# Four slots in place of two for the gated recurrence's results, and the attention's first loads and constants queued four units later

## The chip, the cores and the metric

The kernel runs on one core of a Trainium2 chip. The metric is the device time of one execution in microseconds (us), as the median of several runs. The core has five engines with a queue each: TensorE (PE, with its weight loads shown as PEld), VectorE (DVE), ScalarE (ACT), GpSimd (POOL) and SyncE (SP). SP issues nearly all DMA transfers here. Each engine works through its queue in order.

## The reference

One layer of a streaming encoder on 2048 tokens with 16 meta tokens ahead of them, all in float32, width 1024. Cut to what matters here:

```
p  = rms_norm(h) @ w_in                    # columns: a (gated recurrence), b (attention), c (RWKV-7)
oa = rg_lru_group(xa, ya, ...)             # u = conv4(xa); r, i = sigmoid(u @ ga), sigmoid(u @ gx)
                                           # h_t = a_t h_{t-1} + sqrt(1 - a_t^2) (i u)_t;  h * gelu(ya)
ob = forgetting_attention_group(q, k, v, f_logit, ...)   # softmax(q k / 8 + c_q - c_k), causal, 8 heads
oc = rwkv7_group(pc, ...)                  # matrix-state recurrence, 4 heads of 64
h += rms_norm([oa | ob | oc] @ w_out)
h += rms_norm((gelu(g) * v) @ w_down),  [g | v] = causal_dwconv3(rms_norm(h) @ w_up)
return h without the meta tokens
```

## The kernel before

The program is written as stages, and a list scheduler orders each engine's queue from a simulated timeline, so that small edits move many instructions by a few places. `issue_after(ins)` adds one more rule to that: what is issued inside it stands behind the instruction `ins` in its engine's queue. It is no semaphore.

*Projections.* The input projection runs in three parts ("thirds") of tokens, `w_in_part`. A part has 24 units of 128 output columns, in the order c (8), a (4), k (4), v (4), q (4); each unit loads its weights (`wh`, `wl`, L260) and multiplies them in three products (L193, L194, L195) into a bank `psp`. The bank goes to `stp` (L58, L60) or, for k and q, is split into `sth` (L278) and `stl` (L279), and is stored to DRAM: `scr_p`, `scr_kh`, `scr_kl`, `scr_qh`, `scr_ql`. `core.loaded` is the weight load of the newest unit, `core.split` the newest split L279 on DVE.

*Beside them* the two recurrences run as generators, a step after each unit: the RWKV group (L1106 to L1480; its inverse of small blocks has L1288 on DVE with L1287 on POOL, and the products L1317 with the copies L1333, L1340, L1347 on DVE between) and the gated recurrence, `lru_block`. For each block of 256 tokens and each of two halves of the width `lru_block` loads `lraw` (L1550), writes `u` (tag `lu`, in the profile `rwlu`) on ACT (L1557) and three times on DVE (L1559), multiplies it with the gates, reuses it for the scan, and stores it to `scr_mix` (L1592). The tag has two slots, so a `u` may be written when the store of the `u` two before it has landed. Also beside them, `up_sums` (L1805 loads, sums on POOL, L1811 stores `us`) and, in the middle third, W_out's split.

*The attention* starts when the last third is projected. Its maxima (L645 into `mx`, L650 on DVE into `mc`, L657 `sh`, L660) come first, then the scores (L774, L775). Some of its setup is queued early, in the last third, after a mark set by `SETTLED`: in the loop over units `i` is 1 + the number of units done, one more after the gate's unit,

```
if part == 2 and i == SETTLED:
    core.settled, core.parted = core.loaded.ins, core.split.ins
```

`core.settled` stands on SP's queue: behind it come the loads of the first two heads' keys (`keys`, L605 to L610; only L605 of each can go at once, since the others wait for other tiles or data) and the first three loads of queries (L632). `core.parted` stands on DVE's queue: behind it come the fills of constant rows in these tiles (`fixed`: L567 four times, L559, L560 and L561 three times each). After the attention come W_out and the feed-forward, up and down.

Of the kernel before, what the change touches and what calls it, by code (L numbers as in the profile page):

```python
# [18 lines left out]
P = 128  # L19
# [1516 lines left out]
def lru_block(core, R, scr, k, b):  # L1536

    nc = core.nc
    t0 = max(0, Rwkv.start(b))
    n = min(T, Rwkv.start(b + 1)) - t0  # L1540
    c0 = PAD + t0
    tt = nc.vector.tensor_tensor
    stt = nc.vector.scalar_tensor_tensor

    def tl(s):
        return R.t([P, 256], s, bufs=2 if s == "lu" else 1)[:, :n]

    def raw(row, a):
        t = R.t([P, 260], "lraw", bufs=2)[:, : c0 + n - a]
        nc.sync.dma_start(t, scr["p"][row : row + P, a : c0 + n])  # L1550
        return t

    for p in range(2):
        pc = slice(p, p + 1)
        x = raw(P * p, c0 - 3)
        u, r, g, al = (tl("l" + s) for s in ("u", "r", "g", "a"))
        nc.scalar.activation(u, x[:, 3:], AF.Identity, scale=k["conv_w"][:, 6 + p : 7 + p], bias=k["conv_b"][:, pc])  # L1557
        for i in range(3):
            stt(u, x[:, i : n + i], k["conv_w"][:, 2 * i + p : 2 * i + p + 1], u, op0=ALU.mult, op1=ALU.add)  # L1559


        ps = R.pe()
        pa, px = ps[:, :n], ps[:, 256 : 256 + n]
        nc.tensor.matmul(pa, k["ga_w"][:, p], u, start=True, stop=True)
        nc.tensor.matmul(px, k["gx_w"][:, p], u, start=True, stop=True)
        nc.scalar.activation(r, pa, AF.Abs, bias=k["ga_b"][:, pc])
        nc.vector.tensor_scalar(al, pa, k["ga_b"][:, pc], 0.0, op0=ALU.add, op1=ALU.min)
        nc.scalar.activation(g, px, AF.Tanh, scale=0.5, bias=k["rate"][:, 2, pc])
        nc.scalar.activation(r, r, AF.Tanh, scale=0.5)
        nc.scalar.activation(al, al, AF.Exp)  # L1570
        stt(r, r, 1.0, al, op0=ALU.add, op1=ALU.mult)
        stt(g, g, 1.0, u, op0=ALU.add, op1=ALU.mult)
        yield
        nc.scalar.activation(al, r, AF.Exp, scale=k["rate"][:, 0, pc])
        nc.scalar.activation(r, r, AF.Tanh, scale=k["rate"][:, 1, pc])

        tt(u, al, al, op=ALU.mult)
        stt(r, u, 1.0, r, op0=ALU.add, op1=ALU.mult)
        nc.vector.tensor_scalar(r, r, 1e-34, None, op0=ALU.max)
        nc.scalar.activation(r, r, AF.Sqrt)  # L1580
        stt(g, g, 0.5, r, op0=ALU.mult, op1=ALU.mult)
        nc.vector.tensor_tensor_scan(u, al, g, k["h"][:, pc], op0=ALU.mult, op1=ALU.add)
        nc.vector.tensor_copy(k["h"][:, pc], u[:, n - 1 : n])

        ya, y = raw(2 * P + P * p, c0), r
        nc.scalar.activation(y, ya, AF.Square)
        nc.vector.tensor_scalar(y, y, 0.044715, 1.0, op0=ALU.mult, op1=ALU.add)
        tt(y, y, ya, op=ALU.mult)
        nc.scalar.activation(y, y, AF.Tanh, scale=0.7978845608028654)
        stt(y, y, 1.0, ya, op0=ALU.add, op1=ALU.mult)  # L1590
        stt(u, u, 0.5, y, op0=ALU.mult, op1=ALU.mult)
        nc.sync.dma_start(scr["mix"][P * p : P * p + P, t0 : t0 + n], u)  # L1592
        yield
# [558 lines left out]


READY = 13
SETTLED = 17
PACE = 1.25

WIDE = (0, 5)
# [63 lines left out]
def hybrid_block_kernel(ctx: ExitStack, tc: tile.TileContext, args, out):  # L2222
# [25 lines left out]
    with ExitStack() as p1:  # L2248
# [8 lines left out]
        with ExitStack() as p1a:  # L2257
# [14 lines left out]
            for part in range(3):  # L2272
# [40 lines left out]
                for whole in units:  # L2313
# [10 lines left out]
                    i += 1  # L2324
                    if part == 2 and i == SETTLED:
                        core.settled, core.parted = core.loaded.ins, core.split.ins
# [211 lines left out]
```

## Time and profile before

| | |
|---|---|
| median of 3 runs | 2940.53 us (2938.65 to 2941.93) |
| profiled execution | 2949.89 us, its span 2948.2 us |
| mean granted TensorE clock | 0.979 |
| busy in the span | PE 2844.4, DVE 2006.8, ACT 1502.3, POOL 1297.5 us |
| projections with recurrences | to about 846 us |
| attention, W_out, feed-forward | from 846 us to the end |

Times within the profile are from the start of the span. A row of the timeline has start, duration, engine, line, operation, output<-input, and in brackets how long the engine stood idle before it and what released it. A row of the waits has engine, tile and line, what it waited for, us in total, times, and the longest.

### The profile page before, as it was taken

What the parts mean: (1) busy time and instruction counts of PE and PEld (TensorE: products, weight loads), DVE (VectorE), ACT (ScalarE), POOL (GpSimd) and SP (SyncE); (2) the same over time, 40 slices, a digit from 0 to 9 for tenths busy, and PEclk for the clock granted to TensorE, in tenths of its full rate; (3) what the DMA queues carried; (4) which work ended last, traced back from release to release, by engine and by line L of the source; (5) the groups of instructions that cost most, each with busy time, mean ns of one, the idle gap of its engine ahead of it and who ended that gap; (6) DMA issues with size and microseconds to landing.
All of it is one profiled execution on the core that took longest, in us unless ns stands there. A gap on an engine that the chain in (4) does not pass through costs nothing.

```text
span 2948.2 us, 53211 instructions
## 1 busy us (share of the span) xinstructions
PE 2844.4 (96%) x18854; PEld 2446.0 (83%) x18854; DVE 2006.8 (68%) x3839; ACT 1502.3 (51%) x2937; POOL 1297.5 (44%) x1572
## 2 busy tenths in 40 slices
PE   8999999999988889999999999999999999999998
PEld 8998989888965555666578999999999999787887
DVE  4357655665678875556656988887777787556766
ACT  3246452454436654545645656666666665324333
POOL 1001222222114667677624676456655444656443
PEclk9998999999978999999999999999999999999999
DMA  7775678577643348444264665577777765436453
GB/s 241 250 245 185 215 240 291 174 241 246 204 120 77 90 115 227 97 122 129 48 192 148 212 194 179 160 233 209 219 199 222 215 198 149 141 111 218 151 170 122
DMA packets 470343, 530.51 MB, mean 180 GB/s; under 512 B 86862, under 2 KB 356888, under 8 KB 468524
## 3 DMA queue, kind: packets, MB, share of 16 engines
q1 hardware_dynamic: 469308, 526.18, 59.1%
q8 instruction: 148, 2.42, 0.4%
q0 software_dynamic: 768, 0.93, 0.1%
q14 instruction: 119, 0.97, 0.1%
HBM read 368.07 MB, written 158.90 MB: 179 GB/s over the span
## 4 chain that ended last, share of the span: by engine, by line
PE 75%; DVE 8%; DMA 6%; ACT 5%; issue 3%; POOL 2%; SPq 1%; DVEq 0%; POOLq 0%; ACTq 0%
PE psu L193 9%; PE psu L194 9%; PE psu L195 9%; PE psp L194 4%; PE psp L195 4%; PE psp L193 4%; PE psd L193 4%; PE psd L194 4%; PE psd L195 4%; PE po L797 4%; PE sc L774 2%; PE mx L645 2%; PE pswo L193 2%; PE pswo L194 2%; PE pswo L195 2%
## 5 line engine op out<-in xcount | busy, mean ns | idle before, releaser
L194 PE MATMUL psu<-xo,uw 128*128 128x344 f32 x1848 | 591.5, 320 | 0.0
L193 PE MATMUL psu<-xo,uw 128*128 128x344 f32 x1848 | 586.4, 322 | 3.0 <-DVE vb L1972 2.1
L195 PE MATMUL psu<-xo,uw 128*128 128x344 f32 x1848 | 581.9, 320 | 0.4 <-DVE uw L1781 0.3
L193 PE MATMUL psp<-xh,wh 128*128 128x384 f32 (+2 forms) x1152 | 380.4, 330 | 0.5 <-DMA wh<-scr_wk 0.5
L194 PE MATMUL psp<-xl,wh 128*128 128x384 f32 (+2 forms) x1152 | 375.3, 326 | 0.0
L195 PE MATMUL psp<-xh,wl 128*128 128x384 f32 (+2 forms) x1152 | 373.9, 325 | 0.4 <-DMA wl<-scr_wk 0.4
L1781 DVE TENSOR_TENSOR uw<-uq,uw 128x512 fp32r<-128x512 f32 x341 | 318.2, 938 | 62.5 <-ACT uw L1780 56.5
L193 PEld LDWEIGHTS psu<-xo,uw 128*128 128x128 f32 x1848 | 345.9, 188 | 5.2 <-DVE vb L1972 3.7
L194 PEld LDWEIGHTS psu<-xo,uw 128*128 128x128 f32 x1848 | 347.2, 188 | 0.0
L195 PEld LDWEIGHTS psu<-xo,uw 128*128 128x128 f32 x1848 | 345.7, 188 | 1.1 <-DVE uw L1781 1.1
L1780 ACT ACTIVATE uw<-uq 128x512 fp32r<-128x512 f32 x462 | 287.9, 627 | 95.2 <-PE psu L195 42.0
L779 ACT ACTIVATE p<-sc,bias 128x512 f32<-128x512 f32 (+4 forms) x352 | 197.6, 590 | 168.5 <-PE sc L775 147.5
L650 DVE TENSOR_REDUCE mc<-mx 128x1 f32<-128x512 f32 (+5 forms) x352 | 190.8, 566 | 110.4 <-PE mx L645 78.1
L1920 DVE SCALAR_TENSOR_TENSOR uy<-psu,ffn_cols,uy 128x342 f32<-128x342 f32 (+1 forms) x390 | 220.5, 567 | 61.9 <-ACT uy L1918 60.4
L1928 POOL TENSOR_TENSOR uy<-uy,uy 128x342 f32<-128x342 f32 (+1 forms) x132 | 145.4, 1102 | 231.5 <-ACT uw L1780 56.6
L1781 POOL TENSOR_TENSOR uw<-uq,uw 128x512 fp32r<-128x512 f32 x121 | 183.6, 1518 | 131.9 <-ACT uw L1780 108.8
L193 PEld LDWEIGHTS psp<-xh,wh 128*128 128x128 f32 x1152 | 218.9, 190 | 6.4 <-issue 3.7
L194 PEld LDWEIGHTS psp<-xl,wh 128*128 128x128 f32 x1152 | 219.0, 190 | 5.6 <-issue 4.0
L195 PEld LDWEIGHTS psp<-xh,wl 128*128 128x128 f32 x1152 | 218.9, 190 | 4.9 <-issue 2.9
L818 POOL TENSOR_TENSOR acc<-acc,p 128x512 f32<-128x512 f32 (+3 forms) x186 | 196.1, 1057 | 56.3 <-DVE acc L818 26.8
L1781 DVE TENSOR_TENSOR fo<-u,fo 128x896 fp32r<-128x896 f32 x88 | 100.6, 1143 | 131.0 <-ACT fo L1780 130.5
L1780 ACT ACTIVATE fo<-u 128x896 fp32r<-128x896 f32 x88 | 81.2, 923 | 206.7 <-PE psd L195 118.8
(492 smaller groups left out, 6309.8 us busy)
## 6 DMA issues: line engine op xcount, KB each, us to landing
uq<-scr_us SPq DMA_DIRECT2D x220, 256.0 KB
uq<-in_ffn_up_dram SPq DMA_DIRECT2D x209, 256.0 KB
wh<-scr_wk SPq DMA_DIRECT2D x48, 512.0 KB
wl<-scr_wk SPq DMA_DIRECT2D x48, 512.0 KB
u<-scr_ff SPq DMA_DIRECT2D x88, 256.0 KB
scr_ff<-uy SPq DMA_DIRECT2D x110, 171.0 KB
raw<-in_w_in_dram SPq DMA_DIRECT2D x24, 512.0 KB
scr_wk<-wh SPq DMA_DIRECT2D x24, 512.0 KB
```

The source lines that it names most:

```text
L193: nc.tensor.matmul(out, ah, bh, start=first, stop=False, skip_group_check=more)
L194: nc.tensor.matmul(out, ah, bl, start=False, stop=False, skip_group_check=more)
L195: nc.tensor.matmul(out, al, bh, start=False, stop=last, skip_group_check=more)
L645: nc.tensor.matmul(ps[:rows, : e - a], q3[:, qo : qo + rows], k2[:, a:e], start=True, stop=not last)
L650: self.reduced = nc.vector.tensor_reduce(mc[:rows, i, ci : ci + 1], ps[:rows, : e - a], axis=AX.X, op=ALU.max)
L779: last = nc.scalar.activation(p[:rows, :w], ps[:rows, :w], AF.Exp, bias=bias[:rows, j : j + 1])
L797: mm = nc.tensor.matmul(po[at : at + 64, c0:n], v1[:rows, j], p[:rows, : n - c0], start=start and i < 2, stop=end and i + 2 >= len(group), ...
L818: eng.tensor_tensor(a, ps_[0][0][:rows, c0:n] if start and i == 1 else a, p[:rows, : n - c0], op=ALU.add)
L1780: core.nc.scalar.activation(hi, src, AF.Copy)
L1781: (eng or core.nc.vector).tensor_tensor(lo, src, hi, op=ALU.subtract)
L1920: core.conved = stt(y[:, :n], src[:, i : n + i], cw[:, 44 * i + cc : 44 * i + cc + 1], y[:, :n], op0=ALU.mult, op1=ALU.add)
L1928: core.pooled = nc.gpsimd.tensor_tensor(v[:, :n], g[:, :n], v[:, :n], op=ALU.mult)
```

## The change

It has two edits: four slots for `lu` in place of two (two more tiles of 1 KB per partition), and the mark four units later, after the third v unit in place of the third k unit.

```diff
 def tl(s):
-    return R.t([P, 256], s, bufs=2 if s == "lu" else 1)[:, :n]
+    return R.t([P, 256], s, bufs=4 if s == "lu" else 1)[:, :n]
...
-SETTLED = 17
+SETTLED = 21
```

For DVE the mark moves by one unit alone, to the split of the last k unit, since v units have no split. The scheduler's order changes with it. Numbers behind names are the program's tile numbers; `k_1402` and `q_1403` to `q_1405` are the attention's tiles.

SP's queue in the middle of the last third, before:

```order
L605 DMA k_1402_11222<-scr_kh 64x1040
L632 DMA q_1404_11231<-scr_qh 64x512
L1550 DMA rwlraw_9576<-scr_p 128x256
L289 DMA scr_p<-stp_8355 128x256
L632 DMA q_1405_11235<-scr_qh 64x512
L605 DMA k_1402_11222<-scr_kh 64x1040
L632 DMA q_1403_11227<-scr_qh 64x512
L1550 DMA rwlraw_9626<-scr_p 128x259
L1592 DMA scr_mix<-rwlu_8192 128x256
```

and the same place after:

```order
L1805 DMA us_8822<-in_ffn_up_dram 128x2x128 x3
L1550 DMA rwlraw_9576<-scr_p 128x256
L289 DMA scr_p<-stp_8355 128x256
L1550 DMA rwlraw_9626<-scr_p 128x259
L1592 DMA scr_mix<-rwlu_8192 128x256
```

The two key loads and three query loads are gone from between. They stand some 35 rows further down now:

```order
L1805 DMA us_9467<-in_ffn_up_dram 128x2x128 x4
L605 DMA k_1402_11222<-scr_kh 64x1040
L632 DMA q_1404_11231<-scr_qh 64x512
L632 DMA q_1405_11235<-scr_qh 64x512
L605 DMA k_1402_11222<-scr_kh 64x1040
L632 DMA q_1403_11227<-scr_qh 64x512
L1106 DMA rwraw_9697<-scr_p 128x2x257
L282 DMA scr_kh<-sth_8861 128x256
L283 DMA scr_kl<-stl_8862 128x256
L1811 DMA scr_us<-us_9467 512x1x256
L260 DMA wh_9477<-scr_wk 128x1024
```

Behind them stand a load of the RWKV group, stores of the third k unit, a store of `us` and the weights of unit 20.

DVE's queue at the first of these places, where it takes the `rwlu` of that raw load, before:

```order
L1340 TENSOR_TENSOR rwxf_7542<-rps_7639,rwxu_7503 32x8x32 x4
L60 COPY stp_8383<-psp_8358 128x256
L1288 TENSOR_REDUCE rwix_7467<-rwitmp_7470 128x8
L1559 SCALAR_TENSOR_TENSOR rwlu_9628<-rwlraw_9626,lru_cols,rwlu_9628 128x256
L1288 TENSOR_REDUCE rwix_7467<-rwitmp_7470 128x8
L1347 COPY rwxu_7503<-rps_7704 32x256 x2
```

and after:

```order
L1340 TENSOR_TENSOR rwxf_7542<-rps_7639,rwxu_7503 32x8x32 x4
L60 COPY stp_8383<-psp_8358 128x256
L1559 SCALAR_TENSOR_TENSOR rwlu_9628<-rwlraw_9626,lru_cols,rwlu_9628 128x256
L1288 TENSOR_REDUCE rwix_7467<-rwitmp_7470 128x8
L1559 SCALAR_TENSOR_TENSOR rwlu_9628<-rwlraw_9626,lru_cols,rwlu_9628 128x256
L1347 COPY rwxu_7503<-rps_7704 32x256 x2
```

A second L1559 has come ahead of the copy L1347.

PE's queue from the last product of the projections, before:

```order
L195 MATMUL psp_10174<-xh_6612,wl_9893 128x256
L1413 MATMUL rps_9325<-rstate,rwgt_9300 64x64 x4
L1444 MATMUL rps_9363<-rstate,rwrav_7307 64x64
L1413 MATMUL rps_9325<-rstate,rwgt_9300 64x64 x4
L1444 MATMUL rps_9363<-rstate,rwrav_7307 64x64
L645 MATMUL mx_11279<-k_1402_11222,q_1404_11231 128x144
```

and after:

```order
L195 MATMUL psp_10174<-xh_6612,wl_9893 128x256
L1393 MATMUL rps_9302<-rwsc_7355,rwxu_9238 64x128 x8
L1393 MATMUL rps_9313<-rwsc_7355,rwxu_9238 64x128 x8
L1405 MATMUL rps_9325<-rww_947_7356,rwsc_7355 64x64 x16
L1413 MATMUL rps_9325<-rstate,rwgt_9300 64x64
L645 MATMUL mx_11279<-k_1402_11222,q_1404_11231 128x144
```

L1393 and L1405, which stood among the projections' products before, have come behind the last of them.

DVE's queue at the same place, up to the first L657, before:

```order
L567 CAST k_1411_11247<-ident 64x520 x4
L1454 TENSOR_REDUCE rwgsm_9362<-rps_9363 128x4
L650 TENSOR_REDUCE mc_11277<-mx_11287 128x1
L650 TENSOR_REDUCE mc_11277<-mx_11291 128x1
L1399 COPY rstate<-rstate 128x128
L1198 TENSOR_TENSOR rwrav_9803<-rwr_9796,rwe_9713 128x8x64
L1199 TENSOR_TENSOR rwrav_9803<-rwk_9706,rwe_9713 128x8x64
L1117 SCALAR_TENSOR_TENSOR rwrav_9803<-rwraw_9804,rwkv_cols,rwrav_9803 128x4x64
L1454 TENSOR_REDUCE rwgsm_9362<-rps_9383 128x4
L1117 SCALAR_TENSOR_TENSOR rwrav_9803<-rwraw_9804,rwkv_cols,rwrav_9803 128x4x64
```

and after:

```order
L1417 COPY rstate<-rps_9325 128x128
L567 CAST k_1411_11247<-ident 64x520
L650 TENSOR_REDUCE mc_11277<-mx_11283 128x1
L650 TENSOR_REDUCE mc_11277<-mx_11287 128x1
L1305 STREAM_TRANSPOSE rwxu_10009<-rwxu_10009 128x256
L1417 COPY rstate<-rps_9325 128x128
L650 TENSOR_REDUCE mc_11277<-mx_11291 128x1
L650 TENSOR_REDUCE mc_11277<-mx_11294 128x1
L657 TENSOR_REDUCE sh_11299<-mc_11277 128x4
```

Most of the recurrence's instructions there (L1198, L1199, L1117, L1454) have moved behind L657.

## The prediction

> **What bounds the kernel now.** I read the page first, for the busy times.
>
> ```profile
> PE 2844.4 (96%) x18854; PEld 2446.0 (83%) x18854; DVE 2006.8 (68%) x3839; ACT 1502.3 (51%) x2937; POOL 1297.5 (44%) x1572
> ```
>
> PE is the bound nearly everywhere: only 104 us of the 2948.2 us span (2948.2 - 2844.4) are idle on it, so an edit that touches neither a PE product nor one of those gaps is worth nothing. The windows say where PE stands still or runs at a lower granted clock. The columns are busy us with counts for PE, PEld, DVE, ACT, POOL, then PEclk, the DMA share and GB/s.
>
> ```profile
> 260.00:300.00 40.00, 34.20 (x185) 27.94 (x184) 30.03 (x62) 22.91 (x47) 7.47 (x11) 0.79 0.51 166
> 300.00:400.00 100.00, 99.58 (x944) 91.43 (x943) 62.87 (x154) 48.89 (x92) 23.51 (x37) 1.00 0.70 229
> 720.00:740.00 20.00, 15.60 (x174) 14.05 (x174) 8.27 (x25) 3.77 (x9) 4.76 (x8) 0.74 0.84 253
> 850.00:900.00 50.00, 41.30 (x269) 28.45 (x268) 34.16 (x89) 23.78 (x55) 13.34 (x23) 0.66 0.60 140
> 900.00:1050.00 150.00, 134.32 (x1407) 87.81 (x1407) 123.35 (x341) 94.91 (x208) 88.89 (x145) 0.91 0.34 85
> ```
>
> Three places lose PE time: 260 to 300, 720 to 740, and the attention's start after 850. Each also loses clock. The waits of ACT tie the first two to the slots of `lu`:
>
> ```profile
> ACT rwlu L1557 <- DMA scr_mix<-rwlu: 16.2, 6, 8.2
> ```
>
> ACT's first write of a `u` waited 16.2 us in 6 places for the store of the `u` two before it, at most 8.2 us. The timeline around that longest one, queue by queue:
>
> ```profile
> 721.67 0.53 SPq L1550 DMA_DIRECT2D rwlraw<-scr_p  x1
> 722.51 0.33 SPq L1592 DMA_DIRECT2D scr_mix<-rwlu  x1
> 722.66 0.26 DVE L1288 TENSOR_REDUCE rwix<-rwitmp 128x8 f32<-128x104 f32 x1 [2.19 <-POOL rwitmp L1287]
> 724.42 0.28 PE L194 MATMUL psp<-xl,wh 128*128 128x256 f32 x1
> 725.16 0.27 DVE L1288 TENSOR_REDUCE rwix<-rwitmp 128x8 f32<-128x112 f32 x1
> 726.96 0.60 ACT L1557 ACTIVATE rwlu<-rwlraw,lru_cols 128x256 f32<-128x256 f32 x1 [8.18 <-DMA scr_mix<-rwlu]
> 727.60 0.48 DVE L1559 SCALAR_TENSOR_TENSOR rwlu<-rwlraw,lru_cols,rwlu 128x256 f32<-128x256 f32 x1 [2.17 <-ACT rwlu L1557]
> 728.30 0.88 DVE L1347 COPY rwxu<-rps 32x256 f32<-32x256 f32 x2
> 728.77 0.31 PE L1317 MATMUL rps<-rwxf,rwxu 32*32 32x32 f32 x2 [4.08 <-DVE rwxu L1347]
> ```
>
> It reads as one chain. The store L1592 is issued at 722.51; ACT's L1557 starts at 726.96; DVE, in order, stands at L1559 until 727.60 although the copy L1347 behind it is ready; PE stands 4.08 us for that copy. The windows around it show what follows:
>
> ```profile
> 724.00:728.00 4.00, 0.69 (x7) 0.49 (x5) 1.76 (x6) 0.87 (x2) 1.77 (x4) 1.00 1.03 320
> 728.00:732.00 4.00, 3.23 (x61) 2.88 (x63) 2.62 (x8) 0.75 (x2) 0.52 (x1) 0.52 0.60 205
> 732.00:736.00 4.00, 4.00 (x26) 3.63 (x23) 1.98 (x7) 1.98 (x4) 0.00 (x0) 0.50 0.64 221
> 736.00:740.00 4.00, 4.00 (x32) 3.58 (x33) 0.17 (x1) 0.17 (x1) 0.00 (x0) 0.70 0.99 297
> 740.00:744.00 4.00, 4.00 (x42) 3.54 (x40) 2.67 (x6) 2.69 (x7) 2.65 (x4) 1.00 0.14 42
> ```
>
> After the gap PE is busy at about half clock for some 11 us.
>
> **The change, part by part.** *A, the gap at 724.* Both edits work on it. With four slots L1557 no longer needs the store of `rwlu_8192` but one two `u` older; and the two key loads and three query loads leave SP's queue ahead of the raw load `rwlraw_9626`. What is late next: the raw load itself, issued at 721.67 behind two key loads of 64 x 1040 and three query loads of 64 x 512 numbers, 904 KB, that are gone, so about 3 us sooner (904 KB at the 320 GB/s of the row above). Then L1557 (0.60) is done before 725. On DVE L1288 ends at 725.43; the new order has two L1559 (0.48 each) around it, ahead of L1347, so the copy's first half (0.44) ends at 725.43 + 0.96 + 0.44 = 726.8, and PE, which has stood since 724.69, idles 2.1 us in place of 4.08. DVE's own stand of 2.19 us at 722.66, behind POOL and a load of `us` that shared the transfers with the keys, shrinks too, by 1 us or so as I judge. So 1 us is left and 3.1 us are won. The clock: 0.48 x 3.23 + 0.50 x 4 + 0.30 x 4 = 4.75 us of PE time went at the lower clock in the three windows; with a gap of 1 us I take all of it as won, since no gap of that size is followed by a dip here (300 to 400 has 0.42 us of idle and 1.00, and PE's 0.99 us gap at 716.42 leaves 1.00):
>
> ```profile
> 716.42 1.49 PE L1317 MATMUL rps<-rwxu 32*32 32x32 f32 x96 [0.99 <-ACT stp L58]
> 716.00:720.00 4.00, 3.53 (x114) 3.41 (x115) 3.63 (x12) 2.41 (x5) 1.53 (x3) 1.00 1.12 257
> ```
>
> A = -3.1 - 4.75 = -7.8. Ends: 0 (something else is as late as the store) and -8.8 (4.08 + 4.75).
>
> [...]
>
> *B, the gap at 264 (part 0 to part 1).*
>
> ```profile
> 255.20 0.60 ACT L1557 ACTIVATE rwlu<-rwlraw,lru_cols 128x256 f32<-128x256 f32 x1 [2.21 <-DMA scr_mix<-rwlu]
> 255.83 0.48 DVE L1559 SCALAR_TENSOR_TENSOR rwlu<-rwlraw,lru_cols,rwlu 128x256 f32<-128x256 f32 x1 [1.54 <-ACT rwlu L1557]
> 269.90 0.79 PE L1232 MATMUL rps<-rwrav,rwbk 64*128 64x128 f32 x2 [5.66 <-DVE rwbk L1200]
> 270.00:275.00 5.00, 5.00 (x24) 3.04 (x24) 4.73 (x9) 0.00 (x0) 2.41 (x3) 0.50 0.91 272
> ```
>
> DVE stood 1.54 us at L1559 for the same kind of store and then works almost without a break until the L1200 that PE waits for. Without the stand the whole row moves up 1.5 us, and the PE gap becomes 4.1. That is as long as the gap of A, so I leave the dip behind it as it is: B = -1.5, with ends 0 and -8.7 (if the clock's 0.21 x 34.2 = 7.2 us in 260 to 300 were won too). The remaining 4 of the 6 waits stand in front of no PE gap: 0.
>
> *C, the keys' new place* (SP, about 762). They need about 3 us of transfer, and stand ahead of `rwraw_9697`, an `us` store, and the weights of unit 20:
>
> ```profile
> 768.93 0.38 SPq L260 DMA_DIRECT2D wh<-scr_wk  x1
> 847.97 0.34 PE L645 MATMUL mx<-k,q 128*128 128x144 f32 x1
> 772.00:776.00 4.00, 4.00 (x37) 4.00 (x37) 3.87 (x19) 0.90 (x2) 0.00 (x0) 1.00 1.02 329
> ```
>
> The first product that reads the keys stands at 847.97. The attention follows the last projection there at once, and a unit is some 11 us (part 2's last four cannot start before 802 or so if they end at 846), so unit 20 reads its weights about 30 us after their load. Both have time to spare: 0. Without that cover a late weight load would cost PE its 3 us.
>
> *D, the constants' new place.* DVE's ten fills go behind the `stl` of the last key unit:
>
> ```profile
> 760.69 1.46 DVE L567 CAST k<-ident 64x520 fp32r<-64x520 f32 x4
> 762.20 1.56 DVE L559 MEMSET q<- 64x512 f32 x3
> ...
> 770.89 0.48 DVE L561 MEMSET q<- 1x512 f32 x1 [0.16 <-DVE rstate L1399]
> 780.00:784.00 4.00, 3.91 (x32) 3.55 (x30) 4.00 (x9) 1.41 (x3) 0.00 (x0) 1.00 0.67 211
> ```
>
> 1.46 + 1.56 + 6 x 0.48 = 5.9 us of DVE work leave 760 to 771, where they cost PE nothing, and land at about 773, where DVE is busy 3.87 us of 4 (772 to 776) and then 4.00 (780 to 784). The scheduler answers by setting the recurrences back: in the new order PE has 38 fewer of their instructions behind it at the last projection (1728 in place of 1766). PE has projections to do meanwhile, with five banks between it and DVE: I take +0.5, ends 0 and +3 (half the fills in front of an eviction).
>
> *E, the attention's start.*
>
> ```profile
> 839.19 1.09 PE L1393 MATMUL rps<-rwsc,rwxu 64*64 64x128 f32 x16
> 853.94 0.66 PE L774 MATMUL sc<-q,k 128*128 128x512 f32 x2 [2.18 <-DMA q<-scr_qh]
> 857.71 0.17 DVE L657 TENSOR_REDUCE sh<-mc 128x4 f32<-128x20 f32 x1
> 857.93 1.01 PE L660 MATMUL mx<-ident,sh 128*1 128x128 f32 x4 [3.10 <-DVE sh L657]
> 850.00:855.00 5.00, 2.65 (x39) 1.93 (x38) 4.73 (x12) 0.91 (x2) 0.00 (x0) 0.95 1.05 249
> 855.00:860.00 5.00, 1.57 (x6) 0.91 (x6) 4.33 (x15) 1.30 (x2) 0.00 (x0) 0.50 0.86 207
> ```
>
> PE waits 2.18 us for a query and 3.10 us for DVE's L657, and the clock falls. In the new order about 3 us of DVE recurrence work (L1198, L1199, two L1117, two L1454, L1455s, L1456s: 0.2 to 0.7 each) is behind L657 and not ahead, so L660 can come 2 to 3 us earlier. Against that, 16 L1393, 16 L1405 and an L1413 now stand between the last projection and the first L645, some 2 us of PE by the row of L1393, with a trip over DVE (L1394) between, and DVE's part comes back between 860 and 1050, where DVE is busy 123 of 150 us in 900 to 1050 alone and PE idles 16. I put the two against each other: -2 + 3 = +1, ends -5 and +6.
>
> The sum: -7.8 - 1.5 + 0 + 0.5 + 1 = -7.8 us. The profiled execution took 2949.89 us (span 2948.2 and 1.7 around it), 9.4 over the median of 2940.53, so 2942.1 in its terms; taken off the median, **2932.7 us** (-0.27%).
>
> **The rivals.** *Same (A is small, or E eats it).* Either another work stands behind the store in A (POOL's `us` sums, which DVE's L1288 waits for) and less than 3 us is won, or the projections end 9 us sooner and DVE's backlog in 850 to 1050 takes the time: PE has 16 + 9 us idle there already. A -4, B -1.5, D and E +4: about 2939. For it: the profiled execution is slow against the median, so a typical gap at A may be smaller than this one. Against it: the order takes five transfers from ahead of the raw load.
>
> *Slower.* The late recurrence work makes DVE the bound at the attention's start: if the gap before the first L660 grows by more than 3 us, the low clock (0.34 x 41.3 = 14 us lost in 850 to 900) lasts longer, at half a us for each us. Between the first maximum (L650) and the twentieth the new order has 43 other instructions on DVE where there were 60; 17 at some 0.4 us are 7 us that come later; were all of it waited for, +7, the 2 us of L1393 and L1405, +3 of D and +4 of clock stand against -9.3: +6.7, or 2947. It decides from +15 between 773 and 1050.
>
> *Faster by more.* The gaps at 853.94 and 857.93 shrink until the dip after them does not come: the 14 us of 850 to 900 are won beside the rest: about 2919. [...]
>
> **How the numbers follow.** The forecast 0.50, same 0.23, slower 0.15, more 0.12. A measurement of this kernel can tell about 0.2% (5.9 us) from nothing. The forecast is only 7.8 us, so about 0.10 of its 0.50 falls within that bound: faster 0.40 + 0.12 = 0.52, same 0.33, slower 0.15. The range runs from 2919 (the larger gain) to 2946 (the slower rival short of its end); the likeliest case alone 2927 to 2937.
>
> **What would show it.** In the profile after: at A, ACT's L1557 no longer with a wait for `scr_mix<-rwlu`, PE's L1317 with a gap of under 2 us, PEclk 1.00 from 725 to 740; at B a gap of about 4 us with the dip still there; ACT's total for L1557 on that store near 0; no PE wait on `wh` near 790; the first L660 about 10 us earlier. I am wrong if the 4 us gap only changes its releaser, or if PE's idle in the 200 us after the projections' end grows by more than 8 us.

## The result, and the profile after

The changed kernel took 2967.83 us in the median of 6 runs (2961.89 to 2973.85), against 2939.59 us before (6 runs, 2937.29 to 2956.53): 1.0091 of before, with a 95% interval of 1.0074 to 1.0108. It is slower by about 27 us, where the prediction had 2932.7 and a range to 2946. The profiled execution took 2965.61 us with a span of 2963.9, 15.7 over the span shown of before.

First the head of the page after, busy times of the engines.

```profile
PE 2837.7 (96%) x18854; PEld 2438.2 (82%) x18854; DVE 2003.5 (68%) x3839; ACT 1505.9 (51%) x2937; POOL 1302.0 (44%) x1572
```

PE was busy for 6.7 us less than before (2837.7 against 2844.4) in a span 15.7 us longer, so 22 us of idle time were added. The windows of after that answer to those of before, with the one of before from 740 to 850 ahead of them:

```profile
740.00:850.00 110.00, 106.93 (x1251) 96.67 (x1247) 75.70 (x210) 49.44 (x113) 15.38 (x30) 0.98 0.50 155
```

```profile
260.00:300.00 40.00, 34.15 (x185) 27.94 (x184) 30.00 (x61) 23.18 (x48) 7.58 (x12) 0.79 0.50 169
720.00:740.00 20.00, 18.61 (x237) 16.75 (x237) 10.79 (x31) 6.96 (x17) 5.98 (x11) 0.91 0.76 243
740.00:850.00 110.00, 100.03 (x1132) 91.09 (x1128) 71.70 (x201) 45.95 (x106) 13.75 (x28) 0.97 0.52 157
850.00:900.00 50.00, 38.48 (x269) 26.16 (x269) 33.52 (x90) 21.32 (x51) 16.23 (x27) 0.80 0.70 151
```

The place at 724 got better as forecast: 18.61 us busy in place of 15.60, at 0.91 of the clock in place of 0.74. But 740 to 850, which had lost 3 us (106.93 busy in 110 before), lost 10, of which 8.3 lie ahead of the last projection at 842.1. Neither row explains 15.7 us, let alone 27. A list of landmarks shows more. Answers of the trace on a tile or a line give the first and last start of its instructions; the last projection (L195 on `psp`), the products L696 that the program does once, as its meta tokens' part begins, and the attention's last value product (L797), of before and then of after:

```profile
L195 PE MATMUL psp<-xh,wl x1152: 276/338/582, 21.0 to 845.9; 128*128 128x384 f32 x96, 128*128 128x256 f32 x64, 128*128 128x400 f32 x32
L696 PE MATMUL mx<-mt,mt x8: 173/174/174, 1095.3 to 1095.5; 128*16 128x16 f32 x8
L797 PE MATMUL po<-p,v x704: 204/592/1116, 886.7 to 1494.6; 128*64 128x512 f32 x112, 128*64 128x144 f32 x16, 16*64 16x16 f32 x16, 128*64 128x400 f32 x16
```

```profile
L195 PE MATMUL psp<-xh,wl x1152: 276/337/742, 20.8 to 842.1; 128*128 128x384 f32 x95, 128*128 128x256 f32 x64, 128*128 128x400 f32 x33
L696 PE MATMUL mx<-mt,mt x8: 173/174/176, 1094.9 to 1095.1; 128*16 128x16 f32 x8
L797 PE MATMUL po<-p,v x704: 204/592/1116, 879.9 to 1508.9; 128*64 128x512 f32 x112, 128*64 128x144 f32 x16, 16*64 16x16 f32 x16, 128*64 128x400 f32 x16
```

The projections end 3.8 us earlier. At L696 that lead is down to 0.4. And from L696 to the last L797 the changed kernel needs 414.0 us (1508.9 - 1094.9) in place of 399.3 (1494.6 - 1095.3): 14.7 us in a stretch in which neither edit stands. Behind it the rest takes 1455.0 and 1453.6. Between these two profiles that is almost all: -3.8 + 3.4 + 14.7 + 1.4 = 15.7. Against the medians it is about half of 27 us, since the profile of before is itself 9.4 us over its median, by a stretch ahead of L696, as its second profile shows below. The windows over that stretch, before and after:

```profile
1095.30:1494.60 399.30, 387.73 (x1818) 235.78 (x1817) 239.38 (x494) 212.67 (x389) 263.30 (x355) 0.99 0.47 122
```

```profile
1094.90:1508.90 414.00, 397.12 (x1818) 236.24 (x1817) 241.04 (x494) 213.92 (x389) 265.46 (x355) 0.98 0.45 117
```

PE does the same 1818 products. It idles 16.9 us in place of 11.6, and its products take 9.4 us longer, at a clock of 0.98 in place of 0.99. So more, or worse placed, gaps opened there and the clock fell behind some of them (0.77 from 1180 to 1190, where the kernel before has 1.00).

What differs there? The scheduler gave the attention's second half another order. In the kernel before W_out's first tile stands behind 466 of the attention's products (L645, L774 and L797), in the changed one behind 456, and the next ones behind 507 and not 512, 561 and not 581, 600 and not 637. SP's queue at the place where W_out's weights (L1639) start, before:

```
L862 DMA scr_rden<-dcol_13172 16x32
L635 DMA q_1408_11243<-scr_ql 64x512
L1639 DMA woh<-scr_wo 128x1024
L863 DMA rb_13426<-scr_rden 64x512
L1639 DMA wol<-scr_wo 128x1024
```

and after:

```
L1639 DMA woh<-scr_wo 128x1024
L862 DMA scr_rden<-dcol_13172 16x32
L1639 DMA wol<-scr_wo 128x1024
L1639 DMA woh<-scr_wo 128x1024
L633 DMA q_2078_13586<-scr_qh 64x512
L634 DMA q_2078_13586<-scr_qh 64x512
L863 DMA rb_13426<-scr_rden 64x512
```

`rb` is the attention's reciprocal, which goes out to DRAM (L862) and comes back to 64 partitions (L863); three weight loads of 512 KB stand ahead of its return now, one before. The timeline there, first before:

```profile
1128.06 0.45 SPq L863 DMA_DIRECT2D rb<-scr_rden  x1
1131.89 1.27 POOL L867 TENSOR_TENSOR o<-o,rb 64x512 f32<-64x512 f32 x1 [2.09 <-DMA rb<-scr_rden]
```

and after:

```profile
1129.86 0.45 SPq L863 DMA_DIRECT2D rb<-scr_rden  x1
1136.74 1.28 POOL L867 TENSOR_TENSOR o<-o,rb 64x512 f32<-64x512 f32 x1 [6.13 <-DMA rb<-scr_rden]
1140.46 0.17 DVE L818 TENSOR_TENSOR acc<-acc,p 16x16 f32<-16x16 f32 x1 [5.73 <-POOL acc L818]
1141.28 1.05 PE L645 MATMUL mx<-k,q 128*128 128x512 f32 x2 [2.33 <-DVE mc L650]
```

It took 6.9 us from issue to use (3.8 before). POOL stood 6.13 us for it, DVE 5.73 us for the sums behind it on POOL, and PE 2.33 us for the maximum behind them on DVE. The second execution of the changed kernel (both_again, below) has the same chain:

```profile
1139.46 1.28 POOL L867 TENSOR_TENSOR o<-o,rb 64x512 f32<-64x512 f32 x1 [6.78 <-DMA rb<-scr_rden]
1143.98 1.10 PE L645 MATMUL mx<-k,q 128*128 128x512 f32 x2 [3.02 <-DVE mc L650]
```

three_mark21, with the same order, has 5.92 and 2.18 us. In the ten executions with the old order POOL stands 2.06 to 2.88 us at this place, and PE has no gap of 0.9 us there. A second cluster stands between 1175 and 1183:

```profile
1175.76 0.45 PE L774 MATMUL sc<-q,k 128*128 128x400 f32 x1 [1.19 <-ACT p L779]
1177.67 0.58 PE L645 MATMUL mx<-k,q 128*128 128x384 f32 x1 [1.27 <-DVE mc L650]
1181.30 1.06 ACT L187 ACTIVATE mh<-raw 128x1024 fp32r<-128x1024 f32 x1 [4.46 <-DMA raw<-scr_mix]
1182.89 0.33 PE L774 MATMUL sc<-q,k 128*128 128x144 f32 x1 [1.75 <-ACT p L779]
```

ACT stands 4.46 us for W_out's input `raw`, and PE's next scores wait for the exponentials L779 queued behind it. The wait of ACT is not new. The kernel before has it too:

```profile
1179.10 1.06 ACT L187 ACTIVATE mh<-raw 128x1024 fp32r<-128x1024 f32 x1 [4.32 <-DMA raw<-scr_mix]
```

What is new is that PE stands behind it: the three gaps come to 4.2 us, where the kernel before has one of 1.83 at 1175, ahead of that wait.

### The profile page after: what moved, and what is told of

It is laid out like the page before. It is cut to its first block, busy times and chain, and to the rows that moved or that the text cites. A ratio compares the mean times of both kernels' runs of the same rounds, so it can differ in the third digit from the quotient of the medians.

```text
span 2963.9 us, 53179 instructions
## 1 busy us (share of the span) xinstructions
PE 2837.7 (96%) x18854; PEld 2438.2 (82%) x18854; DVE 2003.5 (68%) x3839; ACT 1505.9 (51%) x2937; POOL 1302.0 (44%) x1572
## 4 chain that ended last, share of the span: by engine, by line
PE 66%; DVE 8%; DMA 7%; ACT 4%; POOL 3%; issue 3%; SPq 1%; DVEq 0%; POOLq 0%; ACTq 0%
PE psu L193 10%; PE psu L194 9%; PE psu L195 9%; PE psd L193 4%; PE psd L194 4%; PE psd L195 4%; PE po L797 3%; PE psp L194 2%; PE psp L195 2%; PE psp L193 2%; PE pswo L193 2%; PE pswo L194 2%; PE pswo L195 2%; PE sc L774 2%; PE mx L645 1%
## 5 line engine op out<-in xcount | busy, mean ns | idle before, releaser
L195 PE MATMUL psu<-xo,uw 128*128 128x344 f32 x1848 | 582.8, 320 | 0.3 <-DVE uw L1781 0.3
L195 PE MATMUL psp<-xh,wl 128*128 128x384 f32 (+2 forms) x1152 | 375.5, 326 | 0.9 <-DMA wl<-scr_wk 0.9
L195 PEld LDWEIGHTS psu<-xo,uw 128*128 128x128 f32 x1848 | 345.9, 188 | 1.1 <-DVE uw L1781 1.0
L779 ACT ACTIVATE p<-sc,bias 128x512 f32<-128x512 f32 (+4 forms) x352 | 197.7, 590 | 160.8 <-PE sc L775 142.0
L650 DVE TENSOR_REDUCE mc<-mx 128x1 f32<-128x512 f32 (+5 forms) x352 | 190.0, 564 | 110.2 <-PE mx L645 76.4
L195 PEld LDWEIGHTS psp<-xh,wl 128*128 128x128 f32 x1152 | 219.3, 190 | 5.7 <-issue 3.6
```

The lines of the kernel that those rows point to most:

```text
L195: nc.tensor.matmul(out, al, bh, start=False, stop=last, skip_group_check=more)
L650: self.reduced = nc.vector.tensor_reduce(mc[:rows, i, ci : ci + 1], ps[:rows, : e - a], axis=AX.X, op=ALU.max)
L779: last = nc.scalar.activation(p[:rows, :w], ps[:rows, :w], AF.Exp, bias=bias[:rows, j : j + 1])
```

## The experiments

Each ratio is over runs of the kernel before on the same chip. The edits:

```diff
 # slots_only:  bufs=4 for "lu";  SETTLED = 17
 # mark_only:   bufs=2;           SETTLED = 21
 # four_mark20, four_mark22, four_mark23: bufs=4; SETTLED = 20, 22, 23
 # three_mark21: bufs=3;          SETTLED = 21
 # two_mark23:  bufs=2;           SETTLED = 23
 # keys21_fills17 (N = 21), keys23_fills17 (N = 23): bufs=4, two marks
-                    if part == 2 and i == SETTLED:
-                        core.settled, core.parted = core.loaded.ins, core.split.ins
+                    if part == 2 and i == N: core.settled = core.loaded.ins
+                    if part == 2 and i == 17: core.parted = core.split.ins
 # hold_wout, on the changed kernel: W_out's weights behind the rb of head 6, block 1
-                queue.dma_start(rb[0][:, :n], ...)
+                self.backs[h, b] = queue.dma_start(rb[0][:, :n], ...)
-            w = w_out_load(core, wp, scr)
+            with tc.issue_after(at.backs[6, 1].ins): w = w_out_load(core, wp, scr)
```

**The edits one by one, and both kernels again.**

> The first edit alone: four slots for lu, the mark as before. Its order of instructions differs from the one before only in the projections (some 1100 of PE's 16436 instructions, most by under 50 places), not in W_out's tiles beside the attention. Theory 1 (the loss comes from the order of W_out's tiles among the attention's second half, which only both edits together change): within 5 us of before, or faster by up to 8 where the gap at 724 goes. Theory 2 (the loss comes from the mark: recurrence set back into the attention's start): the same, -8 to +3. Theory 3 (the four slots cost by themselves): slower by 10 us or more.

> The second edit alone: the mark four units later, two slots. It sets the recurrences back in the last third and permutes the feed-forward's first tiles as both edits together do, but leaves W_out's tiles in the attention's second half where they were. Theory 1 (order of W_out's tiles, both edits together): near before, -8 to +8 us. Theory 2 (the mark's lag at the attention's start): slower by 15 to 28 us, with PE's gap on the next keys near 1086 and the low clock after it.

> The changed kernel once more, on the chip of the two single edits. All theories: 23 to 30 us over before. Its second profile says which of the gaps of the first profile are there in every execution: theory 1 expects gaps and low clock between 1086 and 1260 again (some 14 us against before), theory 2 expects the loss between 842 and 1086.

> The kernel before once more, for a second profile: the first profiled execution took 9.4 us more than the median. If the gap of 4.08 us at 724 with its low clock is a thing of that one execution, this profile has no such gap and takes about 2940; if the gap is in every execution, it is here again and the 9.4 us lie elsewhere.

The slots alone gave 0.9992 (0.9979 to 1.0004), the mark alone 1.0004 (0.9992 to 1.0016), both together 1.0074 (1.0057 to 1.0092). Neither edit costs by itself; the loss belongs to the pair. Theories 2 and 3 in their simple form fall. The kernel before, profiled again, took 2941.01 us and still has the gap at 724 (3.26 us), so the gap is not a thing of one execution; the 9.4 us by which its first profile stood over the median came mostly from elsewhere: 2.5 us by the last projection (843.4 against 845.9) and 6.9 more by L696 (1085.9 against 1095.3), with a clock of 0.83 in place of 0.66 over 850 to 900.

The single edits also say which of the two mends the gap at 724. With four slots alone ACT no longer waits for the store, but for the raw load, which is as late (issued at 722.56, behind the keys):

```profile
727.56 0.60 ACT L1557 ACTIVATE rwlu<-rwlraw,lru_cols 128x256 f32<-128x256 f32 x1 [9.10 <-DMA rwlraw<-scr_p]
729.37 0.31 PE L1317 MATMUL rps<-rwxf,rwxu 32*32 32x32 f32 x2 [3.59 <-DVE rwxu L1347]
```

With the mark alone no gap is left there (PE is busy 20.00 us of 20 in 720 to 740), though ACT waits 15.7 us for stores in all, at most 3.4. So it is the keys that had to go. PE gains nothing by it in all, though: with the mark alone it stands 2.55 us at 716.83 for a copy L58 on ACT, where the kernel before has 0.99, and 2.61 us at 776.27. And the mark alone sets the recurrences back by 22 of PE's instructions at the last projection, not by 38 as both edits do, so it is not quite the test of theory 2 that was expected.

**Other marks.**

> Four slots, the mark at 20 and not 21. The keys, queries and constants go three units later than before, so the recurrences are set back in the last third much as in the changed kernel; but the scheduler's order of the attention's second half is the one before (W_out's first tile behind 466 of the attention's products, not 456). Theory 1 (that order costs 14 to 15 us between the meta products L696 and the last L797): this stretch takes 399 to 400 us again and the kernel is within 8 us of before. Theory 2 (slots and mark together set the recurrences back too far): +15 to +28 us, as the changed kernel.

> Four slots, the mark at 22: keys five units later than before, constants as in the changed kernel or later, and the scheduler's order of the second half is the one before. Theory 1: the stretch from L696 to the last L797 takes 399 to 400 us, the kernel within 8 us of before. Theory 2: +15 us or more, rather more than at 21, since the mark is later still.

> Three slots in place of four, the mark at 21: here the scheduler gives the attention's second half the order of the changed kernel (first W_out tile behind 456 products). Theory 1: the stretch from L696 to the last L797 takes 414 us, the kernel is 20 to 28 us over before, as with four slots. Theory 3 (the fourth slot's memory or place costs): near before.

> Four slots, the mark of SP's queue (keys and queries) at 21, the mark of DVE's queue (fills of constants) left at 17; the second half has the order before. The first prediction's terms A (gap at 724) without D (fills in a dense place of DVE): PE's gap at 724 under 2 us and no wait of PE for rwgsm or stp near 770. If the fills cause the waits at 770 to 776: 4 to 10 us faster than before. If the keys' transfers cause them: the waits stay and the time is within 4 us of before.

Measured: four_mark20 1.0001 (0.9986 to 1.0016), four_mark22 0.9986 (0.9970 to 1.0001), three_mark21 1.0067 (1.0045 to 1.0089), keys21_fills17 0.9987 (0.9971 to 1.0003). Only the kernels with the other order lose, with three slots as with four. The landmarks of all profiled executions (us; "order" is the number of attention products ahead of W_out's first tile):

| kernel | order | last projection | from there to L696 | L696 to last L797 | rest of the span |
|---|---|---|---|---|---|
| before | 466 | 845.9 | 249.4 | 399.3 | 1453.6 |
| before_again | 466 | 843.4 | 242.5 | 399.9 | 1453.5 |
| slots_only | 466 | 845.4 | 248.6 | 399.0 | 1454.2 |
| mark_only | 466 | 846.9 | 245.6 | 399.5 | 1455.5 |
| four_mark20 | 466 | 853.5 | 240.1 | 399.7 | 1452.7 |
| four_mark22 | 466 | 846.3 | 243.9 | 399.2 | 1452.8 |
| keys21_fills17 | 466 | 853.0 | 248.8 | 398.6 | 1452.1 |
| keys23_fills17 | 466 | 846.7 | 235.7 | 397.6 | 1453.2 |
| four_mark23 | 466 | 840.0 | 234.6 | 399.4 | 1454.1 |
| two_mark23 | 466 | 846.6 | 240.4 | 404.8 | 1453.1 |
| after | 456 | 842.1 | 252.8 | 414.0 | 1455.0 |
| both_again | 456 | 844.8 | 254.9 | 414.6 | 1454.2 |
| three_mark21 | 456 | 842.6 | 256.8 | 411.2 | 1456.1 |
| hold_wout | 400 | 842.5 | 259.9 | 407.5 | 1454.9 |

The stretch takes 397.6 to 399.9 us in nine of the ten executions with the old order and 411.2 to 414.6 with the new one. The tenth, two_mark23, has PE's old order there too, but some rows of SP and DVE differ, and its gap at 1172 is 4.49 us where the kernel before has 1.83. The column before it shows a second loss: 252.8 us and more with the new order, 235 to 249 with the old. In that stretch the new order has the recurrences set back: 38 of their instructions fewer at the last projection, and the last one behind 313 of the attention's products in place of 305. In the kernels at 20, 22 and 23, in slots_only and in keys21_fills17 the count at the last projection is the old one or 4 to 5 higher; in mark_only it is 22 lower, with 245.6 us in that column. So both losses go with the new order, which brings two things together: other places for W_out's tiles, and recurrences set back by 38. The traces tell them apart for the larger loss. The recurrences' last store (L1483) is issued at 1079.37 before and at 1078.99 after, and at least 13 us ahead of L696 in every execution, so the stretch behind L696 holds none of their instructions. The 14.7 us there belong to the new order of the attention's second half itself.

**Which part of the mark costs, and a hold on W_out's weights.**

> Four slots, the mark of SP's queue at 23, so that all five key and query loads stand behind the RWKV load rwraw (L1106) and the weights of two more units; DVE's fills at 17 as before; the second half has the order before. If the waits at 770 to 782 come from rwraw standing behind the keys: ACT's wait at L1116 near 770 falls from 7 to 8 us to about 2.5, as in the kernel before, PE's wait on stp there goes, and the kernel is 4 to 9 us faster than before. If they come from the transfers themselves, wherever they stand: PE still waits 3 us or more somewhere in 765 to 800, and the time is within 4 us of before.

> Four slots, one mark at 23 for both queues: keys behind rwraw, and the fills behind the last key unit's split, in the dense place of DVE; the second half has the order before. Beside the kernel with keys at 23 and fills at 17 it tells what the fills cost: if they cost PE 3 us as in the changed kernel (wait at L1178 for rwgsm), this one is 2 to 5 us slower than that; if not, both are equal.

> The changed kernel, with W_out's weight loads (L1639) held in SP's queue behind the attention's load of reciprocals rb (L863) that they stood ahead of. W_out's tiles get other places too (the first behind 400 products). Theory 1a (part of the 14.8 us is POOL standing 6 us at L867 for rb, whose round trip runs beside 8 MB of W_out's weights, with DVE and PE behind it): L867's wait near 1136 falls to 2 to 4 us, PE's wait of 2.3 to 3.0 us for L650 there goes, the stretch from L696 to the last L797 takes 409 to 412 us in place of 414. Theory 1b (only the places of W_out's tiles matter): the stretch keeps 414 or more, though that wait goes.

> Two slots as before, the mark at 23 for both queues: the faster version found (four slots, mark 23: 0.9969 of before) without its four slots. If the slots carry part of the gain (ACT's wait at L1557 for the store of rwlu, with DVE's L1347 and PE's L1317 behind it): 0.998 to 1.001 of before, with L1557 waiting 15 us or more for stores in all. If the mark alone carries it, since the raw load is then no longer behind the keys: 0.996 to 0.998, as with four.

keys23_fills17 took 0.9983 (0.9967 to 0.9999), four_mark23 0.9969 (0.9954 to 0.9984), two_mark23 0.9982 (0.9970 to 0.9994). The fills in their late place do not cost 2 to 5 us: four_mark23, which has them there, is not the slower of the first two. keys21_fills17, without the late fills, still has PE standing 3.47 us at 781.40 for DVE's copy L60 behind the late `rwraw`, so its second case held: the waits stay, and the time is 3.8 us from before. What the keys cost the RWKV group depends on where its load L1106 of `rwraw` stands. ACT's wait for it near 770, before, in the changed kernel, with the keys at 22, and with the keys at 23 and the fills at 17:

```profile
777.64 0.51 ACT L1116 ACTIVATE rwwa<-rwraw,rwkv_om 128x256 f32<-128x256 f32 x1 [2.81 <-DMA rwraw<-scr_p]
```

```profile
767.91 0.51 ACT L1116 ACTIVATE rwwa<-rwraw,rwkv_om 128x256 f32<-128x256 f32 x1 [7.29 <-DMA rwraw<-scr_p]
```

```profile
764.56 0.51 ACT L1116 ACTIVATE rwwa<-rwraw,rwkv_om 128x256 f32<-128x256 f32 x1 [2.25 <-DMA rwraw<-scr_p]
```

```profile
774.36 0.51 ACT L1116 ACTIVATE rwwa<-rwraw,rwkv_om 128x256 f32<-128x256 f32 x1 [6.38 <-DMA rwraw<-scr_p]
```

Behind the keys it waited 5.3 to 8.1 us in every kernel at 20 or 21 whose mark moved; ahead of them 2.25 (four_mark22), 2.60 (four_mark23) and 1.41 (two_mark23). In four_mark23 the group's next load stands behind the keys, and ACT waits 6.63 us for that one at 783.80 (3.81 before), with no gap of PE over 0.5 us between 765 and 795. The last row is a miss: there the load stands ahead of the keys but is issued at 768.12 only, behind another unit's weights, and ACT waits 6.38 us anyhow. four_mark23 is faster than both kernels of this study, by 0.31% (0.16% to 0.46%); whether its four slots add anything to two_mark23's 0.18% (0.06% to 0.30%) the intervals do not tell.

hold_wout, on the changed kernel, took 1.0044 (1.0027 to 1.0061), where the changed kernel had 1.0074 and 1.0091:

```profile
1137.97 1.26 POOL L867 TENSOR_TENSOR o<-o,rb 64x512 f32<-64x512 f32 x1 [1.80 <-DMA rb<-scr_rden]
1141.48 1.01 PE L193 MATMUL pswo<-woh,mh 128*2 128x512 f32 x2 [2.89 <-DMA woh<-scr_wo]
```

POOL's wait for `rb` fell from 6.13 to 1.80 us, PE's wait for L650 there went, and the stretch fell to 407.5 us, with 2.89 of that a new wait for the held weights. So theory 1a fits, with a larger gain than it claimed. But W_out's tiles moved as well (the first behind 400 products), and no run tells the hold and the move apart. About 8 us over the old order's 397.6 to 399.9 are left.

## Why the prediction was wrong, step by step

**A, the gap at 724: right in its size, in part wrong in its cause.** PE's gap is now 0.96 us, 3.1 less, as worked out:

```profile
725.02 0.24 PE L1317 MATMUL rps<-rwxf,rwxu 32*32 32x32 f32 x2 [0.96 <-DVE rwxu L1347]
728.00:732.00 4.00, 4.00 (x24) 3.62 (x23) 1.68 (x7) 1.34 (x3) 0.00 (x0) 0.67 0.65 210
732.00:736.00 4.00, 4.00 (x45) 3.49 (x45) 1.28 (x5) 1.49 (x4) 0.31 (x1) 1.00 0.90 279
```

The dip shrank but did not vanish, though the prediction took all of it as won: 0.67 in the first of these two windows. PE's first L1393 behind that place starts at 737.42 in place of 743.74, 6.3 us earlier where 7.8 was forecast. In the second execution of the changed kernel the gap is 0.49 us without a dip, but PE stands 1.94 us at 721.59 for a copy L58 on ACT, where the two executions of the kernel before have 0.99 and 1.22. But only the mark did it: with the slots alone the raw load was as late as the store.

**B, the gap at 264: wrong, small.** PE's L1232 starts at 269.47 in place of 269.90, because another DVE instruction now ends last. -0.4 in place of -1.5.

**C, the keys' new place: the first step that failed.** I set it to 0, by the time that unit 20's weights and the keys themselves had to spare. The list of what stands behind the keys named `rwraw_9697`, and I did not price it. ACT, which takes it in order, stood 7.29 us (2.81 before), and PE's transposes 2.32 us for a copy behind it on ACT (the first row):

```profile
769.71 0.44 PE L297 MATMUL psv<-ident,stp 128*128 128x128 f32 x2 [2.32 <-ACT stp L58]
776.33 1.09 PE L1178 MATMUL eps<-ident,rwe 128*128 128x128 f32 x4 [3.35 <-DVE rwgsm L79]
775.00:780.00 5.00, 3.67 (x18) 3.71 (x19) 4.72 (x14) 1.42 (x3) 0.00 (x0) 0.51 0.66 213
```

PE's gaps of over 0.6 us between 760 and 800 come to 5.7 us here, to 6.2 in the second execution, and to 3.3 to 6.2 in the variants with `rwraw` behind the keys (mark_only, four_mark20, three_mark21, keys21_fills17). They come to 0 to 2.7 us in the variants with `rwraw` ahead of them, and to nothing with the keys in their old place. So the late load, with what stands behind it, came to 3 to 6 us of PE's time, where the sum had 0 for it.

**D, the fills: its top end here, but not by itself.** The second row is a wait behind the fills in the changed kernel: 3.35 us where I had +0.5 with an end at +3, and the clock at 0.51 behind it. DVE, too, had stood 6.3 us for that load, so that the fills (769.46 to 777.8) and the recurrence's small steps to `rwgsm` came together, one between the other. In four_mark23 the same wait is 1.04 us, and keys21_fills17 stands 3.47 us at the late load without any fill there, so the 3.35 us are not the fills' own price. By the last projection the lead is 3.8 us of A's 6.3, and that with 38 of the recurrences' instructions still to do.

The clock does not go by the length of a gap alone here. The second execution of the changed kernel has the same gap of 3.35 us ahead of the same L1178, at 781.19, and one of 2.87 us at 774.57, and its clock is 1.00 in each window from 770 to 800; its 1.94 us at 721.59 leave 1.00 from 720 to 740 as well. In the first execution 3.35 us went with 0.51, and even the gap of 0.96 us was followed by a fall, though PE idled in smaller pieces beside it too (3.04 us busy of 4 from 724 to 728). So the prediction's view that a gap of about 1 us is followed by no dip did not hold. The spells differ as well: in the clock records of the traces, half clock lasts 3.41 us behind the gap of 0.96 us (from 727.27), 6.83 us with the one of 3.35 (from 775.05, within it) and 10.24 us with the one of 4.08 in the kernel before (from 728.17, within it).

**E, the attention's start: mis-sized.** The first L660 starts at 857.11, 0.8 us earlier and not 10. From the last projection to L696 I had +1 with an end at +6; the three executions of both edits, or of three slots at 21, took 252.8 to 256.8 us where the seven of the kernel before and the other variants up to mark 22 took 240.1 to 249.4, so about +9. PE's idle in the 200 us behind the last projection grew by 5.5 us alone (30.8 against 25.3), so the prediction's own sign, 8 us there, would not have shown it. Part of it is a wait that I had not seen: the next key load stands behind the recurrences' last store in SP's queue, and PE, earlier there, waited longer:

```profile
1085.88 1.31 PE L645 MATMUL mx<-k,q 128*128 128x400 f32 x3 [6.65 <-DMA k<-scr_cl]
```

(2.07 us before.) This wait is 5.8 to 6.7 us in all four executions with the new order and at most 2.8 in the ten with the old. That the recurrences' lag is the cause of the rest is argued from the order and from these spans; a lag of 38 instructions was not tried apart from the new order, and one of 22 (mark_only) brought no such loss.

**What was missing altogether** is a term behind 1086. This is the step that cost most: the sum ended with the attention's start, since neither edit stands later, so it put the attention's second half at nothing, and 14.7 us went there, with another order of W_out's tiles and PE behind POOL's late `rb`. The rival "slower" had the right sign, by another mechanism at another place, and a chance of 0.15.

What stays open is the other 8 us of the second half's loss, after the hold on the weights. The cluster at 1175 to 1183 is hardly it, since hold_wout has one gap of 1.56 us there. Counted from the same value product (at 1319.4 before, 1328.1 in the changed kernel, 1329.9 in hold_wout) to the last one, the kernels take 175.2, 180.8 and 180.0 us, at a clock of 1.00 and with four more products in the later two. So about 5 us of it lie that late, part of them work that moved there. Open, too, is why the scheduler turns to the other order at mark 21 with three, four or five slots, and at no other mark from 17 to 23 with four (five slots and the marks 18 and 19 were not run).

## What to carry to other kernels

Where a scheduler orders the program from a simulated timeline, a small edit can have, beside its local price, another one far away by a new order: compare the order of every engine to the end of the program, by landmarks that each kernel has once, before the sum is closed; a neighbouring value of the same number (23 in place of 21) kept a gain of 0.31% and not the loss. When transfers move in an in-order queue, price each load that they are put ahead of by the engine that takes it, not by the cover of the moved ones. And of two edits at one gap, ask which of them alone would close it.

## What the hardware showed that I had not expected

A 64x512 broadcast load took 6.9 us from issue to use with three 512 KB loads ahead of it, 3.8 with one and 4.3 with none (hold_wout, issued at 1133.69), so the count of loads ahead does not set it alone. And two executions of one kernel differ by 9.4 us at L696 with the same instructions, with 0.86 and 0.88 of the clock from the last projection on:

```profile
845.90:1095.30 249.40, 215.32 (x1927) 139.70 (x1925) 190.28 (x517) 138.90 (x306) 131.33 (x213) 0.86 0.44 105
```

```profile
843.40:1085.90 242.50, 211.26 (x1928) 136.95 (x1927) 187.75 (x517) 138.68 (x306) 132.04 (x213) 0.88 0.45 108
```

In the fastest kernel here the same stretch took 234.6 us at 0.92. So this one stretch moves by 7 us between two executions of one kernel, nearly as much as the whole forecast.
